# Layer 0 feed-forward: seven block products for gate and up, and a separate down pass

## The chip, the cores and the metric

The kernel runs on one core of a Trainium2 chip. The metric is the device time of one execution in microseconds. Engines are named as in the profile: PE (TensorE), PEld (its weight loads), DVE (VectorE), ACT (ScalarE), POOL (GpSimd), SP (the queue that issues all DMAs here).

## What is computed

Two layers over 512 latent tokens and 256 context tokens of width 1024, in fp32. Layer 0 mixes with differential attention, layer 1 with grouped-query attention; each is followed by a SwiGLU feed-forward with 2816 hidden columns, and adaLN shifts, scales and gates come from small sums over `ada_w`:

```python
def swiglu(t, w_gu, w_down):
    gate, up = jnp.split(t @ w_gu, 2, axis=-1)
    return (jax.nn.silu(gate) * up) @ w_down

mod = (cond_lat @ ada_w[i] + ada_b[i])         # six vectors per layer; modc the same for the context
x  = x  + g1 * y                               # y from the mixer
x  = x  + g2 * swiglu(modulate(rmsnorm(x, norm2_g[i]), sh2, sc2), ffn_w_gu[i], ffn_w_down[i])
xc = xc + cg2 * swiglu(modulate(rmsnorm(xc, norm2_g[i]), csh2, csc2), ffn_w_gu[i], ffn_w_down[i])  # not in the last layer
```

## The kernel before

Tokens are held in blocks of 128: latent blocks 0 to 3, context blocks 4 and 5, worked through in the order 4, 5, 0, 1, 2, 3. For accuracy every fp32 matrix is split in two parts, a rounded high part (an ACT cast to fp32r) and the rest, the low part (a subtraction on DVE or POOL), and each product is three matmuls: high x high, high x low, low x high (`mm3`, L99). `split` (L85) casts on ACT and subtracts on POOL; `split_psum` subtracts on DVE.

The instruction order on each engine is made when the program is built: a scheduler simulates the program in the order of the source and fills the in-order queues; `tc.issue_after(x)` keeps instructions behind x on their engine. All DMAs go through one queue, L55.

The layer-0 feed-forward is `ffn` (L369). It goes through 22 chunks of 128 hidden columns in 11 pieces of two. For each chunk, `stage` loads 1 MB of gate/up weights into one of three raw buffers and splits them (128x2048 on ACT and POOL), and `gu_mm` (L426) computes gate and up transposed: the weights stand in the array, the tokens stream, 512 latent columns into `psgu` and 256 context columns into `psgc`, over 8 blocks of the contraction and 3 products each: 48 pairs of matmuls a chunk. ACT applies silu, DVE multiplies by up, ACT and DVE split the result. One piece later, `down` (L375) multiplies the 256 hidden values of a piece by their rows of `w_down`: for 6 token blocks and 2 column halves, 6 matmuls of 512 columns into one of two `psP` banks, then DVE multiplies by the gate (L386) and adds to the residual `xt` (L387): 132 evictions. While this runs, `ada_job` (L395) makes the adaLN sums of layer 1: twelve column blocks of 512, each from two 1 MB loads, with DVE accumulations (L223, L225) per contraction block, two sums (latent, context) for the first four column blocks and one for the other eight; then small matmuls (L239, L251) and their evictions (L241, L252).

Before it, `out_proj` (L350) adds the attention output to `xt`; after each token block `after` starts the norm (`norm_a`, L292: Square on ACT, a reciprocal root with DVE steps of 128x1, a scaling), and one block later `norm_b` (L330) transposes on PE, modulates on DVE and ACT (L322, L324), and splits (L327, L328). The last two blocks' norms are done by `mid`, inside the first chunk. After the feed-forward, `g_weights` (L1011) has split the key/value weights of layer 1 into the buffers `c` and `d`, and `g_proj` multiplies block after block by them (`psgkv`).

PSUM has eight banks: `psS` twice two, `psP` two, `psT` two. SBUF pools are stacks at two sides; pool `h0p` at the right holds the buffers c, d and e, two of 8 KB a partition each, 48 KB a partition in all, in which the input of the first projection, the attention output and then the feed-forward's weight splits live.

## Time and profile before

| | us |
|---|---|
| median of three runs | 1748.36 |
| lowest, highest | 1746.21, 1749.71 |
| span of the profiled execution | 1742.5 |
| of it: layer-0 feed-forward, first gate/up matmul to first key/value matmul of layer 1 | 606.4 |
| PE, DVE, POOL, ACT busy, share of the span | 95%, 71%, 44%, 39% |

The profiled execution's own time is not shown beside its span; the three runs lie 4 to 7 us above the span. A matmul's busy time includes the end of its pipeline and so overlaps its neighbours'; the distance from start to start says what a matmul costs in a stream. A row's idle time is that of the engine just before the instruction, with what ended it.

### The profile page before, as it was taken

The page shows a single profiled execution, that of the slowest core. Times are in us where ns is not written, and L with a number is a line of the kernel's source. Part 1 is how long each engine was busy: PE and PEld are TensorE (multiplying, and loading weights), DVE is VectorE, ACT ScalarE, POOL GpSimd, SP SyncE. Part 2 cuts the span into 40 slices and gives each one's busy share as a digit, 9 for nine tenths or more (in the row PEclk, how much of TensorE's full clock was granted, in tenths as well). Part 3 has the DMA queues.
Part 4 walks back from the last instruction along what each step waited for, and adds up shares of the span by engine and source line. Part 5 has one row for each costly group of instructions (what it writes and reads, how often), then busy time and mean ns, then how long its engine had stood idle before and what let it go on. Part 6 is the DMA issues. An engine that isn't in the chain of part 4 may idle for free.

```text
span 1742.5 us, 23575 instructions
## 1 busy us (share of the span) xinstructions
PE 1657.0 (95%) x8934; PEld 1403.6 (81%) x8934; DVE 1237.5 (71%) x2016; ACT 673.0 (39%) x1491; POOL 767.6 (44%) x702
## 2 busy tenths in 40 slices
PE   5899999989998999999999999999999999999998
PEld 2789899975778888887777888778897888888887
DVE  4777888877484488878777555798883467677676
ACT  4667767677444121111211022364673522222120
POOL 2687666664645242223232233174435344354340
PEclk8899999999999999999999999999999999999999
DMA  8311111129523133355333221021203133233311
GB/s 303 102 55 38 46 46 58 34 75 336 195 73 121 49 121 111 107 169 169 122 119 99 73 73 40 25 74 48 73 25 120 36 105 103 73 97 99 95 49 49
DMA packets 162435, 165.81 MB, mean 95 GB/s; under 512 B 5097, under 2 KB 120186, under 8 KB 162322
## 3 DMA queue, kind: packets, MB, share of 16 engines
q1 hardware_dynamic: 162322, 164.31, 29.5%
q8 instruction: 70, 1.15, 0.3%
q14 instruction: 43, 0.35, 0.1%
HBM read 159.81 MB, written 4.48 MB: 94 GB/s over the span
## 4 chain that ended last, share of the span: by engine, by line
PE 68%; DVE 18%; ACT 4%; DMA 4%; POOL 3%; issue 2%; SPq 0%; DVEq 0%; ACTq 0%; POOLq 0%
PE psgu L433 24%; PE psgc L433 5%; PE psd L100 5%; PE psd L102 5%; PE psd L101 5%; DVE adacc L225 3%; DMA adaw<-in_ada_w_dram 3%; PE psp L100 2%; PE psp L102 2%; PE psp L101 2%; DVE adacc L223 2%; DVE x L387 2%; DVE xd L386 1%; PE pso L100 1%; PE pso L102 1%
## 5 line engine op out<-in xcount | busy, mean ns | idle before, releaser
L93 POOL TENSOR_TENSOR gul<-gu,guh 128x2048 fp32r<-128x2048 f32 x44 | 211.6, 4809 | 419.6 <-ACT guh L86 419.6
L386 DVE TENSOR_TENSOR xd<-psd,gate 128x512 f32<-128x512 f32 x220 | 151.1, 687 | 202.7 <-PE psd L102 202.5
L387 DVE TENSOR_TENSOR x<-x,xd 128x512 f32<-128x512 f32 x220 | 274.4, 1249 | 5.5
L86 ACT CAST guh<-gu 128x2048 fp32r<-128x2048 f32 x44 | 83.9, 1906 | 403.8 <-PE psgu L433 234.4
L91 POOL TENSOR_TENSOR dl<-wd,dh 128x1024 fp32r<-128x1024 f32 x44 | 120.9, 2768 | 146.1 <-ACT dh L86 146.1
L433 PE MATMUL psgu<-h3latl,guh 128*128 128x512 f32 (+1 forms) x384 | 144.5, 377 | 1.1 <-POOL h3latl L328 1.1
L433 PE MATMUL psgu<-h3lath,gul 128*128 128x512 f32 (+1 forms) x384 | 144.4, 376 | 0.0
L433 PE MATMUL psgu<-h3lath,guh 128*128 128x512 f32 (+1 forms) x384 | 144.3, 377 | 0.0
L433 PE MATMUL psgu<-h2lath,guh 128*128 128x512 f32 (+1 forms) x368 | 142.1, 386 | 0.0
L433 PE MATMUL psgu<-h2lath,gul 128*128 128x512 f32 (+1 forms) x368 | 141.8, 385 | 0.0
L433 PE MATMUL psgu<-h2latl,guh 128*128 128x512 f32 (+1 forms) x368 | 141.8, 385 | 0.0
L100 PE MATMUL psd<-dh,ah 128*128 128x512 f32 x264 | 106.0, 402 | 16.2 <-DVE xd L386 12.1
L102 PE MATMUL psd<-dh,al 128*128 128x512 f32 x264 | 104.8, 397 | 0.0
L101 PE MATMUL psd<-dl,ah 128*128 128x512 f32 x264 | 104.5, 396 | 0.0
L433 PE MATMUL psgc<-h2ctxh,gul 128*128 128x256 f32 x352 | 100.2, 285 | 0.4 <-POOL gul L93 0.4
L433 PE MATMUL psgc<-h2ctxh,guh 128*128 128x256 f32 x352 | 100.1, 284 | 0.0
L433 PE MATMUL psgc<-h2ctxl,guh 128*128 128x256 f32 x352 | 99.6, 283 | 0.0
L225 DVE SCALAR_TENSOR_TENSOR adacc<-adaw,cond,adacc 128x512 f32<-128x512 f32 x112 | 97.5, 896 | 1.3
L100 PE MATMUL psp<-dwh,h0lath 128*128 128x384 f32 x256 | 88.9, 347 | 7.6 <-DVE vl L97 7.6
L101 PE MATMUL psp<-dwl,h0lath 128*128 128x384 f32 x256 | 88.9, 347 | 0.0
L102 PE MATMUL psp<-dwh,h0latl 128*128 128x384 f32 x256 | 88.8, 347 | 0.0
L433 PEld LDWEIGHTS psgu<-h3latl,guh 128*128 128x128 f32 x384 | 72.2, 188 | 15.8 <-POOL h3latl L328 1.3
(389 smaller groups left out, 4669.1 us busy)
## 6 DMA issues: line engine op xcount, KB each, us to landing
adaw<-in_ada_w_dram SPq DMA_DIRECT2D x48, 1024.0 KB
gu<-in_ffn_w_gu_dram SPq DMA_DIRECT2D x88, 512.0 KB
wd<-in_ffn_w_down_dram SPq DMA_DIRECT2D x22, 1024.0 KB
dw<-in_diff_w_in_dram SPq DMA_DIRECT2D x48, 256.0 KB
x<-in_x_dram SPq DMA_DIRECT2D x8, 512.0 KB
wo<-in_diff_w_out_dram SPq DMA_DIRECT2D x4, 1024.0 KB
gw<-in_gqa_w_in_dram SPq DMA_DIRECT2D x4, 1024.0 KB
wo<-in_gqa_w_out_dram SPq DMA_DIRECT2D x4, 1024.0 KB
```

Source lines behind the costliest of these rows:

```text
L86: S.copy(hi, src)
L91: G.tensor_sub(lo[:, ns], src[:, ns], hi[:, ns])
L93: G.tensor_sub(lo[:, :, ns], src[:, :, ns], hi[:, :, ns])
L100: PE.matmul(ps, lhi, rhi, start=start, stop=False)
L101: PE.matmul(ps, lhi, rlo, start=False, stop=False)
L102: PE.matmul(ps, llo, rhi, start=False, stop=stop)
L223: V.tensor_scalar(acc, w[:, k, :], c, None, op0=ALU.mult)
L225: V.scalar_tensor_tensor(acc, w[:, k, :], c, acc, op0=ALU.mult, op1=ALU.add)
L386: V.tensor_mul(tmp, ps, gates[g][:, s, cs])
L387: last_v[0] = V.tensor_add(xt[tb][:, cs], xt[tb][:, cs], tmp)
L433: last[0] = PE.matmul(o, w_[:, k, us], act.t[kind][x_].k(k, sl_), start=(k == 0 and x_ == 0 and w_ is whi), stop=(k == KC - 1 and w_ is wlo))
```

## The change

Layer 1 is left as it is; layer 0's feed-forward is written anew as two passes.

First pass (`ffn_up`). The tokens are two halves of 384 columns, blocks 4, 5, 0 and blocks 1, 2, 3. For each chunk, the 2x2 blocks of weights (gate and up, by lower and upper half of the contraction) times the 2x2 blocks of activations (contraction half by token half) are computed by seven products of sums instead of eight (Winograd's form of Strassen's scheme). `Forms` makes the seven activation forms once: b11, b21 (first half), b22, and the sums t1 to t4, which need both halves, each split in high and low; the forms take the place of the attention output and of other buffers. `prep` makes the seven weight forms of a chunk, seven products ahead: four sums or differences of 128x512 on POOL, seven ACT casts, six low parts on DVE and one on POOL. Each product is 12 matmuls of 384 columns. Four of the products add on to one PSUM bank, with ACT copies (c1, c2) and a DVE addition (u2) between; DVE adds the copies, multiplies silu(gate) by up, and the result goes to DRAM (`a0`) unsplit. The adaLN sums move into this pass: one step every two products (`ada_step`), with loads of half the size into two buffers of their own.

Second pass (`ffn_down`). For each half, all 22 chunks are added up in six PSUM banks, and each of the 12 results is evicted once. Activations are read back from DRAM and split (128x1536), the weights of down are loaded and split for each half. Norms of layer 1 follow the blocks of each half.

Buffers change with it: `h0p` becomes two 24 KB tiles, used in turn by the projection's input, the attention output, the forms t1 to t4 and at last the activations of down (`a2t`, in the place of t1 and t2, held until the last matmul of down). Only then the pool with c, d, e opens in the same 48 KB, in the order c, e, d; the key/value weights go to e and d, so the first high part lies within `a2t`'s 24 KB.

```diff
+    class Forms:
...
+        def put(self, name, j, src, eng):
...
+            S.copy(t[:, 0, :, cs], src)
+            last_v[0] = eng.tensor_sub(t[:, 1, :, cs], src, t[:, 0, :, cs])
...
+        def done(self, xs, tb, banks=None):
+            ht = norm_mod(xs, norm_t(xs, tb, self.l, 1, banks), tb, self.l, 1)
...
+            if half == 0:
+                self.put("b11", j, lo, V)
+                self.put("b21", j, hi, G)
+            else:
+                b11, b21 = self.ht[0, j]
+                self.put("b22", j, hi, G)
+                V.tensor_sub(b11, lo, b11)
+                self.put("t1", j, b11, V)
+                V.tensor_sub(lo, hi, lo)
+                V.tensor_sub(hi, hi, b11)
+                self.put("t2", j, hi, G)
+                V.tensor_sub(b21, b21, hi)
+                self.put("t3", j, lo, V)
+                self.put("t4", j, b21, G)
...
+    RHS = {1: "b11", 2: "b21", 3: "b22", 4: "t4", 5: "t1", 6: "t2", 7: "t3"}
+    PLEAD = 7
+
+    def product_order():
+        o = [(0, 1), None, (0, 2), (1, 1), (1, 2), None, (2, 1), (2, 2), (0, 5), (0, 6), (0, 3), (0, 7), (1, 5), (0, 4), (1, 6), (1, 3), (1, 7)]
+        o += [(1, 4), (2, 5), (2, 6), (2, 3), (2, 7)]
+        for h in range(3, NHC):
+            o += [(h, 1), (h - 1, 4), (h, 2), (h, 5), (h, 6), (h, 3), (h, 7)]
+        return o + [(NHC - 1, 4)]
+
+    def ffn_up(l, F, ev_tile, st_tile, a_dram, adds, mid, step):
...
+        def prep(hc, n):
+            w = raw[hc]
+            r11, r12, r21, r22 = [w[:, k : k + 4, u : u + P] for u in (0, P) for k in (0, 4)]
+            s1 = st_tile(hc)
+            if n == 5:
+                adds[0].tensor_add(s1, r21, r22)
+                adds[1].tensor_sub(r21, r11, r21)
+            elif n == 6:
+                adds[2].tensor_sub(r11, s1, r11)
+            elif n == 3:
+                adds[3].tensor_sub(r12, r12, r11)
+            src = {1: r11, 2: r12, 5: s1, 6: r11, 3: r12, 7: r21, 4: r22}[n]
...
+            S.copy(t[:, 0], src)
+            (G if n == 4 else V).tensor_sub(t[:, 1], src, t[:, 0])
+            if n == 4:
+                load(hc + 3)
...
+            for k in range(4):
+                for a_, b_ in ((0, 0), (0, 1), (1, 0)):
+                    last_m[0] = PE.matmul(
+                        ps, w[:, a_, k, :], x[:, b_, k, :],
+                        start=(n in (1, 2, 5) and k == 0 and a_ + b_ == 0),
...
+            if n == 1:
+                S.copy(c1, ps)
+            elif n == 2:
+                V.tensor_add(g1, ps, c1)
+                S.activation(g1, g1, AF.Silu)
+            elif n == 5:
+                S.copy(c5, ps)
+            elif n == 6:
+                S.copy(c2, ps)
+            elif n == 3:
+                V.tensor_add(g2, ps, c2)
+                S.activation(g2, g2, AF.Silu)
+            elif n == 7:
+                V.tensor_add(u2, ps, c5)
+                last_v[0] = V.tensor_mul(g2, g2, u2)
+                puts.append((i, hc, 1, g2))
+            else:
+                last_v[0] = V.tensor_mul(g1, g1, ps)
+                puts.append((i, hc, 0, g1))
+            step(i)
...
+    def ffn_down(l, xt, halves, g, a_dram, a_tile, banks, lo_eng, after):
...
+        PREP, LOAD, TAIL = 3, 5, 2
...
+            for k in range(NHC - TAIL):
+                load(half * NHC + k + LOAD)
+                for tb in tbs:
+                    for ch in range(2):
+                        mms(k, tb, ch)
+                prep(half * NHC + k + PREP)
...
+                    V.tensor_mul(tmp, ps[tb][ch], gates[g][:, s, cs])
+                    last_v[0] = V.tensor_add(xt[tb][:, cs], xt[tb][:, cs], tmp)
+                    after(tb, ch)
...
+    HALVES = ([4, 5, 0], [1, 2, 3])
...
+    def ada_work(js):
...
+            for k0 in range(0, KC, 2):
+                w = half_slab(f"adw{j}_{k0}").rearrange("p (k n) -> p k n", k=2)
+                dma(w, ada_w[1, k0 * P : (k0 + 2) * P, j * 512 : j * 512 + 512].rearrange("(k p) n -> p k n", p=P))
+                yield
+                with tc.issue_after(last_v[0].ins):
...
+    def ada_step(i):
+        while ada_n[0] < (i - 14) // 2:
+            ada_n[0] += 1
+            next(ada_it, None)
...
-    ffn(0, xt, h2, tb_order, (0, 1), tags0, lambda: after(None, True), lambda: gate_load(1), [mk_ada1(j) for j in (0, 1, 2, 3, 6, 7, 8, 9, 4, 5, 10, 11)], after0)
...
+    ffn_up(
+        0, F0, ev0, lambda hc: st0[:, hc % 2], a0, (G, G, G, G), mid0, ada_step)
...
+    ffn_down(
+        0, xt, HALVES, (0, 1), a0, lambda i: a2t[:, i % 2 * 8 * TH : i % 2 * 8 * TH + 8 * TH],
+        (("S", "S", "P"), ("T", "S", "S")), G, lambda tb, ch: after(tb) if ch else None)
...
-        wt = g_weights(GQA_HEADS * GQA_DH, "kv", "cd")
+        wt = g_weights(GQA_HEADS * GQA_DH, "kv", "ed")
```

## Rows read from the trace of the kernel before

**Rows 1.** Busy shares of the page; a window: us, busy by engine, clock, DMA share.
```profile
PE 1657.0 (95%) x8934; PEld 1403.6 (81%) x8934; DVE 1237.5 (71%) x2016; ACT 673.0 (39%) x1491; POOL 767.6 (44%) x702
...
522.75:1129.19 606.44, 583.16 (x3091) 493.13 (x3090) 419.07 (x518) 120.78 (x165) 179.93 (x55) 0.99 0.32 100
```

**Rows 2.** Timeline of PE (start, us, what): the stage's first matmul, layer 1's first.
```profile
522.75 0.36 PE L433 MATMUL psgc<-h2ctxh,guh 128*128 128x256 f32 x1
...
1129.19 0.47 PE L100 MATMUL psgkv<-gwhkv,h1ctxh 128*128 128x512 f32 x1
```

**Rows 3.** Timeline of PE: ends of a run of gate/up pairs, of down matmuls, of 384-column matmuls.
```profile
559.97 0.39 PE L433 MATMUL psgu<-h2lath,gul 128*128 128x512 f32 x1
...
583.14 0.39 PE L433 MATMUL psgu<-h2lath,gul 128*128 128x512 f32 x1
...
584.42 0.39 PE L100 MATMUL psd<-dh,ah 128*128 128x512 f32 x1
...
586.99 0.39 PE L102 MATMUL psd<-dh,al 128*128 128x512 f32 x1
...
153.10 0.34 PE L102 MATMUL psp<-dwh,h0latl 128*128 128x384 f32 x1
...
155.35 0.33 PE L100 MATMUL psp<-dwh,h0ctxh 128*128 128x384 f32 x1
```

**Rows 4.** PE's waits: by line in the stage, in the timeline, and in the table of waits.
```profile
L100 PE MATMUL psd<-dh,ah 128*128 128x512 f32 x264 | 106.0, 402 | 16.2 <-DVE xd L386 12.1 <-DVE mod L241 4.1
...
533.67 1.97 PE L307 MATMUL pt<-ident,xs01f 128*128 128x128 f32 x8 [4.87 <-DVE m_n L112]
...
PE psd L100 <- DVE xd L386: 12.1, 10, 2.2
```

**Rows 5.** Down's evictions by tile, 520 to 1130: ns min/median/max, first and last start.
```profile
L386 DVE TENSOR_TENSOR xd<-psd,gate x132: 676/691/694, 586.0 to 1129.1; 128x512 f32<-128x512 f32 x132
L387 DVE TENSOR_TENSOR x<-x,xd x130: 676/692/5061, 587.0 to 1127.8; 128x512 f32<-128x512 f32 x130
```

**Rows 6.** Timelines of DVE and POOL where they meet (start, us).
```profile
525.99 3.26 DVE L105 TENSOR_TENSOR m_n<-m_n,r_n 128x1 f32<-128x1 f32 x1 [1.21 <-ACT r_n L114]
...
524.19 5.04 POOL L93 TENSOR_TENSOR gul<-gu,guh 128x2048 fp32r<-128x2048 f32 x1
...
1132.33 5.00 POOL L328 TENSOR_TENSOR h1ctxl<-xs10f,h1ctxh 128x512 fp32r<-128x512 f32 x1 [7.10 <-ACT h1ctxh L327]
...
626.77 8.04 DVE L225 SCALAR_TENSOR_TENSOR adacc<-adaw,cond,adacc 128x512 f32<-128x512 f32 x12
```

**Rows 7.** Durations by tile (min/median/max) and, the last row, by line.
```profile
L328 POOL TENSOR_TENSOR h2latl<-xs01f,h2lath x2: 1274/1284/1294, 537.8 to 541.0; 128x512 fp32r<-128x512 f32 x2
...
L91 POOL TENSOR_TENSOR dl<-wd,dh x22: 2331/2756/3116, 521.8 to 1064.0; 128x1024 fp32r<-128x1024 f32 x22
...
L479 DVE TENSOR_TENSOR sil<-sil,psgc x22: 404/413/423, 545.1 to 1102.3; 128x256 f32<-128x256 f32 x22
...
L86 ACT CAST gwhkv<-gwkv 128x512 fp32r<-128x512 f32 x8 | 4.5, 615 | 31.8 <-PE psgu L433 31.8
```

**Rows 8.** adaLN: chain of work (start, us), and DVE's waits for its loads.
```profile
635.04 1.34 PE ps_adac L239 x12
...
912.50 0.96 PE ps_adar L251 x2
...
741.87 6.27 DMA adaw<-in_ada_w_dram
...
DVE adacc L223 <- DMA adaw<-in_ada_w_dram: 12.6, 3, 5.9
```

**Rows 9.** Timeline of DVE: first and last of the norms' steps at the start.
```profile
509.74 0.75 DVE L297 TENSOR_SCALAR xs01g<-x,r_n 128x1024 f32<-128x1024 f32 x1
...
541.50 1.37 DVE L328 TENSOR_TENSOR h2latl<-xs01f,h2lath 128x512 fp32r<-128x512 f32 x1 [1.45 <-ACT h2lath L327]
```

**Rows 10.** POOL's splits of the key/value weights by tile.
```profile
L91 POOL TENSOR_TENSOR gwlkv<-gwkv,gwhkv x8: 1287/1301/1834, 1073.6 to 1105.8; 128x512 fp32r<-128x512 f32 x8
```

More of the change, by code (lines that the diff above doesn't have):

```diff
@@ L298, in norm_a, with norm_t @@
         return xs
-    def norm_t(xs, tb, l, which):
+    def norm_t(xs, tb, l, which, banks=None):
         pts = []
@@ new lines, in finish_to @@
+    def finish_to(l, which, act):
+        return lambda xs, tb: norm_b(xs, tb, l, which, *act.blk(tb))
+    HALVES = ([4, 5, 0], [1, 2, 3])
+    TH = 3 * P
+    form_view = lambda t: t.rearrange("p (x k n) -> p x k n", x=2, k=4)
+    F0 = Forms(0, HALVES, {
+        n: form_view(bfp.tile([P, 8 * TH], F32R, tag=n, name=f"hf0{n}", bufs=1)) for n in ("b11", "b21", "b22")})
+    after = mk_after(0, 1, lambda tb: mp.tile([P, D], F32, tag="m", name=f"xs01{tb}") if tb not in (2, 3) else half_slab(f"xs01{tb}"), lambda xs, tb: F0.done(xs, tb, "T" if tb in (2, 3) else None), 1, NLAT - 1)
```

269 lines of the change are left out of this document (225 added, 44 removed).

## The prediction

> **What bounds the kernel now.** I read the page's busy shares first, then the windows by stage, then TensorE's timeline inside the stage that the diff rewrites, and last its idle time and what ends it. The page gives PE 95% of the span [rows 1]; busy matmul time overlaps itself, so pitches (start to start) tell more. Layer 0's feed-forward runs from its first gate/up matmul at 522.75 us to the first matmul of layer 1 at 1129.19 us: 606.4 us, a third of the span, at a granted clock of 0.99, the 2.4 GHz level [rows 1, 2]. In a quiet stretch the pair of a 256-column and a 512-column matmul repeats 66 times between 559.97 and 583.14, 0.351 us a pair; eleven steps of the down matmuls take 2.57 us, 0.2336 us each [rows 3]. One hidden chunk (128 hidden columns) has 48 pairs, 16.85 us; 22 of them make 370.7 us. Down has 11 x 12 x 6 = 792 matmuls, 185.0 us. So 556 of the 606 us are matmuls at their own pitch: the stage is bound by TensorE. The other 50 us are adaLN matmuls, transposes, a 4.9 us wait for the last norms at the start, and waits of down for its PSUM evictions (16.2 us of idle before L100) while DVE does adaLN sums [rows 4].
>
> **What is removed and added on TensorE.** Gate and up become seven products instead of eight blocks. A product is 4 x 3 matmuls of 384 columns, so 22 x 7 x 12 = 1848. The same form exists in the q/k/v projections: thirteen steps from 153.10 to 155.35 are 2.25 us, 0.1731 us each [rows 3]. That is 2.08 us a product, 14.54 us a chunk and 319.9 us in all, 50.8 us less than 370.7. Per column 384 is no worse than the old mix (0.451 ns against 0.457). Down keeps its 792 matmuls: 185.0 us. The adaLN matmuls stay: twelve records in 1.34 us, so 96 make 10.7 us, and two row matmuls in 0.96, so eight make 4 us [rows 8]. Forty transposes stay too: eight took 1.97 us with a wait inside [rows 4], so 10 us at most; I take 5. The floor of the new stage is 319.9 + 185.0 + 14.7 + 5 = 525 us, 82 us below 606. All that follows is how much of the 82 is lost again.
>
> **Down's evictions.** Before, 132 times a multiplication from PSUM and an addition to x, 0.69 us each at the median [rows 5]: 182 us of DVE. After, twelve pairs, 17 us. The 16.2 us of idle are gone with them, and this is part of the 82. In their place down loads and splits its weights twice. A 128x1024 subtraction took POOL 2.76 us (median) and TensorE now needs 18 x 0.2336 = 4.2 us for one chunk of one half, so POOL, the slowest of the splitters, is covered with 1.4 us to spare [rows 7]; three chunks of lead cover the loads. I cost this at nothing; without cover it would be 2.8 us at each half.
>
> **The port between DVE and POOL.** This is the main loss. In the trace a DVE instruction on SBUF operands waits while POOL runs one: a 128x1 multiplication took 3.26 us under a 5.04 us POOL subtraction, and a POOL subtraction that takes 1.29 us took 5.00 us under a DVE chain [rows 6]. The DVE multiplications that read PSUM never stretch (676 to 694 ns), the SBUF additions do (up to 5061 ns) [rows 5]. So SBUF work of DVE and POOL adds up; only PSUM-reading DVE work runs beside POOL.
> Ten products in the new loop, 20.8 us on TensorE, cost DVE: 8.6 lo parts of 128x512 at 0.61 (pitch: 0.69 less the overlap of neighbours) = 5.2; evictions of 384 columns, between the 413 ns of 256 and the 691 of 512 [rows 5, 7], 0.475 at pitch, five a chunk = 3.4, of which 2.7 read PSUM. POOL: five instructions of 1.29 us a chunk = 9.2 [rows 7]. The adaLN sums advance by one of twelve column blocks in ten products. The first four blocks carry two sums: 14 accumulations at 0.67 (twelve took 8.04 us) and two starts, 10.3; the other eight carry one, 5.1 [rows 6].
> First four blocks: 5.2 + 3.4 + 10.3 = 18.9 for DVE, with POOL 28.1 if nothing overlaps, 25.4 if all PSUM reads do; TensorE needs 20.8 + 1.7 for adaLN = 22.5. Loss 2.9 to 5.6 per block, 12 to 22 in all. The lead of seven weight preparations does not absorb it, because evictions stand in the same DVE queue: u2 must have left PSUM before the eighth step of the chunk may add to it, one product later. I take 12, since PSUM reads do overlap in the rows.
> Other eight blocks: 13.7 + 9.2 = 22.9, or 20.2 with overlap, against 21.7. So 0 to 10. In addition a half-size adaLN load has only two products (4.2 us) from issue to use. Before, a 1 MB load cost 6.3 us where the chain shows it, and DVE waited three times, 12.6 us [rows 8]. I add up to 8 and take 6 for both together, nearest to half of the 12.6.
> The Trainium skill, page "SBUF — State Buffer", section "SBUF: two separate sides", says that DVE and POOL hold their shared ports exclusively for a whole instruction, and counts DVE instructions with two SBUF inputs among the holders. The rows agree (3.26 and 5.00 us). By that rule the first four blocks cost 12 us and not 0, and the rule speaks against moving more DVE and POOL work beside each other, as this change does.
>
> **The start.** Six products (12.5 us) and two blocks' transposes (2 us) are there to cover the norms of token blocks 2 and 3, so TensorE reaches the first product that needs the second half at about 537. Between 509.74 and 542.87 DVE does some 22 us of norm work in the kernel before, the rest is idle or locked out by POOL's big splits [rows 6, 9]. After, the same stretch has five more 128x512 steps for each of three blocks (9.2), ten lo parts of weights (6.1) and first evictions (1.4): 39 us, so 549. POOL's fifteen short subtractions (19 us), 11 of them beside PSUM reads, add up to 8. The stall is 6 (if block 1's forms fit into idle time) to 22; I take 14. Before's own 4.9 us there is inside the 606.
>
> **The joints.** Up to down: weights and activations of the first chunks can be split some products early, and the last PSUM bank frees in one eviction; 2 us (0 to 6). Between the halves and at the end: 2 (0 to 4). Down to layer 1: before, the key/value weights were split at 1073 to 1106, well ahead. After, their first tile lies in memory that the down activations hold until the last matmul. Four subtractions of 1.30 us [rows 10] then run one by one while TensorE wants 0.7 us a piece, so about 4 us (0 to 8).
>
> **The sum.** 82 - 14 - 12 - 6 - 2 - 2 - 4 = 42 us. The span of 1742.5 becomes 1700; the runs shown are 1746 to 1750, some 4 to 7 us around the span, which the change doesn't touch. So 1748.4 - 42 = 1706 us.
>
> **The rivals.**
> 1. All hidden. The scheduler orders the queues so that the port is shared without loss and the forms are ready. Only the 6 us at the start stay: 82 - 6 = 76, 1672; with a little at the joints 1680. For: eight of the twelve adaLN blocks need 20.2 against 21.7 with overlap. Against: the first four exceed TensorE even then. Chance 0.17.
> 2. The port binds the whole first pass. Nothing overlaps: 22 + 10 + 8 for the pass, 22 at the start, 7 at the joints: 69, leaving 13: 1735. Chance 0.18. By the skill's rule on the shared ports nothing but PSUM reads runs beside POOL, so the rule stands between this rival and the forecast.
> 3. Slower: in-order queues chain the products. Each chunk reuses one PSUM bank for five products, with ACT copies (c1, c2) and DVE additions (u2) between them, and the same queues hold weight casts that wait for POOL. If a cast that waits for POOL stands ahead of a copy, TensorE waits in every chunk. Before, a down matmul waited 1.2 us on average and up to 2.2 for DVE's eviction, ten times [rows 4]. With the 22 us of start and joints, the remaining 60 us are used up at 0.39 us a product. Two waits of 2 us in each of 22 chunks are 88 us: 1748 - 82 + 22 + 88 = 1776. For: the bank is reused within one product's time (2.08 us). Against: ACT has seven casts of 128x512 (615 ns [rows 7]) and five passes of 384 columns, at most 0.6 each, 7.3 us in 14.5, and preparations run six products ahead. Chance 0.12.
>
> **How the numbers follow.** Forecast (1688 to 1724) 0.50, all hidden 0.17, port-bound 0.18, slower 0.12, and 0.03 for landing within 0.2% (3.5 us, about what a measurement of this kernel can tell from no change). Faster 0.85, same 0.03, slower 0.12. For 8 in 10 the range takes in most of the first and second rival: 1674 to 1744. It leaves out the slower case and the very best.
>
> **What would show it.** In the profile after, chunk period on TensorE without adaLN near 14.5 us and 384-column pitch 0.173 us; if the period is longer in quiet chunks too, rival 3. In the first four adaLN blocks longer periods, with DVE additions and POOL instructions stretched beyond 0.69 and 1.29 us; if they stretch but TensorE doesn't idle, rival 1. One idle stretch of 6 to 22 us on TensorE after six products, ended by DVE or a form. Down at 0.2336 us without idle. A gap of up to 8 us at the first psgkv, ended by a split. The prediction is wrong if the loss per chunk is the same with and without adaLN, or if DMA ends most idle time.

## The result, and the profile after

The changed kernel takes 1728.57 us (median of four runs, 1725.67 to 1733.0) against 1748.46 before; the ratio is 0.9883 with a 95% interval of 0.9859 to 0.9908. So 20 us were gained where 42 were forecast. The sign is right and the time lies inside the range, but less than half of the forecast gain came. The profiled execution has a span of 1723.9 us against 1742.5, 18.6 us less, and its own time is 1725.67.

First the borders of the stage, from TensorE's timeline of the kernel after (start, us, what): the first product, the first key/value matmul, the first gate/up matmul of layer 1.

```profile
530.37 1.13 PE L634 MATMUL psu<-hf0b,wf 128*128 128x384 f32 x5
...
1100.94 0.71 PE L100 MATMUL psgkv<-gwhkv,h1ctxh 128*128 128x512 f32 x2
...
1347.65 0.48 PE L489 MATMUL psgu<-h3lath,guh 128*128 128x256 f32 x2
```

Against [rows 2] the 18.6 us divide into four parts.

| stretch | before, us | after, us | difference | forecast |
|---|---|---|---|---|
| start to the stage's first product | 522.75 | 530.37 | +7.6 | 0 |
| the stage, to the first key/value matmul | 606.4 | 570.6 | -35.9 | -46 |
| key/value projection and attention of layer 1 | 235.8 | 246.7 | +10.9 | +4 |
| the rest (layer 1's feed-forward) | 377.5 | 376.2 | -1.3 | 0 |

Next the windows inside the first pass (us from the span's start, length, busy us with instruction counts of PE, PEld, DVE, ACT, POOL, the granted clock of TensorE as a share of 2.4 GHz, DMA share, GB/s).

```profile
530.00:560.00 30.00, 17.33 (x94) 15.89 (x92) 30.00 (x48) 19.41 (x45) 19.98 (x14) 0.78 0.24 71
560.00:600.00 40.00, 35.39 (x186) 34.56 (x187) 26.76 (x33) 15.12 (x30) 25.51 (x15) 0.91 0.39 112
600.00:640.00 40.00, 37.59 (x199) 36.45 (x198) 36.95 (x46) 13.86 (x28) 15.88 (x11) 0.91 0.46 138
640.00:680.00 40.00, 38.11 (x219) 37.34 (x217) 39.76 (x53) 13.92 (x28) 19.12 (x12) 0.96 0.54 157
...
800.00:840.00 40.00, 40.00 (x221) 37.77 (x221) 37.01 (x49) 16.53 (x33) 19.20 (x13) 1.00 0.61 183
```

TensorE idles 17.3 us at the start (530 to 573) and 8.7 us in the rest of the pass, nearly all of that before 741. DVE is full from 530 to 560 and nearly full again to 720, where the adaLN blocks with two sums run. From 760 on only one wait of 0.4 us is left, though adaLN blocks with one sum run there. Up to 720 the clock's mean is below 1.00 in every window: TensorE has four stretches at the lower level, 0.50 or 1.2 GHz (columns as above).

```profile
546.88:567.36 20.48, 9.09 (x32) 7.78 (x31) 18.07 (x31) 13.07 (x27) 15.78 (x9) 0.50 0.19 53
618.56:625.39 6.83, 6.83 (x26) 6.83 (x26) 3.78 (x7) 1.98 (x4) 1.30 (x1) 0.50 0.28 90
649.28:652.69 3.41, 3.41 (x12) 3.41 (x11) 3.41 (x7) 0.66 (x2) 0.63 (x1) 0.50 1.07 319
683.42:686.83 3.41, 3.41 (x12) 3.41 (x13) 3.41 (x7) 0.53 (x1) 1.18 (x1) 0.50 0.86 277
```

The first begins behind a wait of 2.2 us and has the waits of 7.1 and 3.7 in it; the others follow waits of 1.2, 0.4 and 0.8, of 0.4 and 0.8, and of 4.0 us. TensorE works 9.1 us in the first and 13.7 in the others, all of it at half speed, so 4.5 us are lost at the start and 6.8 in the rest of the pass.

The waits of TensorE in this pass by what ended them (us in total, times, longest), in answer to [rows 4]:

```profile
PE pt L319 <- DVE xs L334: 7.1, 1, 7.1
PE psu L634 <- DVE g L658: 4.0, 1, 4.0
PE psc L634 <- ACT tf L360: 3.7, 1, 3.7
PE psu L634 <- POOL tf L361: 2.8, 1, 2.8
PE ps_adac L248 <- DVE adacc L1231: 2.7, 4, 0.8
```

And what TensorE does undisturbed, from its timeline: one product begins 2.08 and 2.12 us after the one before. [Rows 3] gave 2.08.

```profile
895.10 2.24 PE L634 MATMUL psu<-tf,wf 128*128 128x384 f32 x12
897.18 2.28 PE L634 MATMUL psu<-hf0b,wf 128*128 128x384 f32 x12
899.30 2.10 PE L634 MATMUL psc<-hf0b,wf 128*128 128x384 f32 x11
```

Down's 132 evictions are twelve now (by tile: ns min/median/max, first and last start), and TensorE waits 1.8 us for them in all, where [rows 4] had 12.1, or 16.2 with the adaLN steps in DVE's queue:

```profile
L739 DVE TENSOR_TENSOR xd<-psd,gate x12: 673/684/692, 993.7 to 1099.9; 128x512 f32<-128x512 f32 x12
```

At the border to layer 1 stands a gap that was not there before. In order of time, from the timelines of POOL, DVE, ACT and PE:

```profile
1100.34 11.96 POOL L91 TENSOR_TENSOR gwlkv<-gwkv,gwhkv 128x512 fp32r<-128x512 f32 x8 [4.92 <-ACT gwhkv L86]
1105.06 2.96 DVE L1371 TENSOR_TENSOR gtab<-rope 128x256 f32<-128x256 f32 x2
1112.68 0.20 ACT L113 ACTIVATE r_n<-m_n 128x1 f32<-128x1 f32 x1 [5.12 <-DVE m_n L112]
1115.42 1.09 PE L319 MATMUL pt<-ident,xs 128*128 128x128 f32 x8 [2.83 <-DVE xs L306]
1117.94 0.38 ACT L1303 COPY gtemp<-psgkv 128x256 f32<-128x256 f32 x1
1118.19 0.40 ACT L96 CAST vvh<-psgkv 128x256 fp32r<-128x256 f32 x1
1125.33 1.72 DVE L344 TENSOR_TENSOR h1latl<-xs,h1lath 128x512 fp32r<-128x512 f32 x1 [2.45 <-ACT h1lath L343]
1128.18 0.74 DVE L97 TENSOR_TENSOR vvl<-psgkv,vvh 128x256 fp32r<-128x256 f32 x2
1128.73 0.77 PE L100 MATMUL psgkv<-gwhkv,h1lath 128*128 128x512 f32 x1 [10.42 <-DVE vvl L97]
```

The two PSUM banks of `psgkv` hold blocks 4 and 5. ACT's copy out of the first of them stands in its queue behind the norm steps of the last blocks, and DVE's `vvl` behind their low parts. In the longer gap DVE itself idles 3.8 us, 2.45 of it for ACT's cast of a last block, while `vvl`, whose input `vvh` was cast at 1118.2, stands behind: what holds the bank is the place of `vvl` in the queue. TensorE idles 2.8 and 10.4 us, and its next twelve matmuls start 0.43 us apart instead of 0.23, the lower clock level, until 1133.99, which costs another 2.5 us. That is 15.7 us of loss in one place.

### The profile page after: what moved, and what is told of

Same layout as the page of the kernel before. It is cut to its first block, busy times and chain, and to the rows that moved or that the text cites. A ratio compares the mean times of both kernels' runs of the same rounds, so it can differ in the third digit from the quotient of the medians.

```text
span 1723.9 us, 23682 instructions
## 1 busy us (share of the span) xinstructions
PE 1618.3 (94%) x8622; PEld 1411.0 (82%) x8622; DVE 1200.6 (70%) x1979; ACT 775.8 (45%) x1710; POOL 893.1 (52%) x818
## 4 chain that ended last, share of the span: by engine, by line
PE 73%; DVE 14%; ACT 4%; POOL 3%; DMA 3%; issue 3%; SPq 0%; DVEq 0%; ACTq 0%; POOLq 0%
PE psgu L489 14%; PE psu L634 10%; PE psd L102 5%; PE psd L101 5%; PE psd L100 5%; PE psc L634 4%; DVE adacc L1231 2%; PE psp L100 2%; PE psp L102 2%; PE psp L101 2%; DMA adaw<-in_ada_w_dram 2%; PE pso L100 2%; PE pso L102 1%; PE pso L101 1%; DVE wf L604 1%
## 5 line engine op out<-in xcount | busy, mean ns | idle before, releaser
L93 POOL TENSOR_TENSOR gul<-gu,guh 128x2048 fp32r<-128x2048 f32 x22 | 102.2, 4645 | 181.5 <-ACT guh L86 181.5
L634 PE MATMUL psu<-tf,wf 128*128 128x384 f32 x756 | 144.8, 340 | 4.8 <-POOL tf L361 2.8
L443 DVE TENSOR_TENSOR x<-x,xd 128x512 f32<-128x512 f32 x88 | 143.9, 1637 | 2.3
L100 PE MATMUL psp<-dwh,h0h 128*128 128x384 f32 x384 | 134.1, 349 | 11.4 <-DVE vl L97 8.6
L634 PEld LDWEIGHTS psu<-tf,wf 128*128 128x128 f32 x756 | 133.4, 190 | 7.0 <-POOL tf L361 3.1
L101 PE MATMUL psp<-dwl,h0h 128*128 128x384 f32 x384 | 133.3, 347 | 0.0
L102 PE MATMUL psp<-dwh,h0l 128*128 128x384 f32 x384 | 132.9, 347 | 0.0
L1231 DVE SCALAR_TENSOR_TENSOR adacc<-adw,cond,adacc 128x512 f32<-128x512 f32 x112 | 116.7, 1058 | 6.2 <-DMA adw<-in_ada_w_dram 5.9
L604 DVE TENSOR_TENSOR wf<-gu,wf 128x512 fp32r<-128x512 f32 x110 | 104.7, 965 | 5.4 <-ACT wf L603 5.4
L634 PE MATMUL psu<-hf0b,wf 128*128 128x384 f32 x504 | 99.1, 344 | 4.0 <-DVE g L658 4.0
```

Of the source, the lines that this page charges most:

```text
L93: G.tensor_sub(lo[:, :, ns], src[:, :, ns], hi[:, :, ns])
L100: PE.matmul(ps, lhi, rhi, start=start, stop=False)
L101: PE.matmul(ps, lhi, rlo, start=False, stop=False)
L102: PE.matmul(ps, llo, rhi, start=False, stop=stop)
L443: last_v[0] = V.tensor_add(xt[tb][:, cs], xt[tb][:, cs], tmp)
L604: (G if n == 4 else V).tensor_sub(t[:, 1], src, t[:, 0])
```

## The experiments

Each edit is shown against the kernel it was made on. "First pass" is from the start of the first product to the start of the last, "projection" from the first key/value matmul to the last, "attention" from there to layer 1's first gate/up matmul; all are from TensorE's timeline of the profiled execution, and for the kernel after they are 383.9, 53.2 and 193.5 us. Before the change the projection took 40.5 and the attention 195.4.

**The changed kernel again.** No edit.

> The changed kernel once more, unaltered. It tells what of its 7.6 us before the feed-forward is of the kernel and what of one execution: last output-projection matmul at 529 us against 522 before. Theory (a property of its instruction order): the 2.7 us that stand between 184 and 408 us and the 5 us more at the joint of attention and output projection come back within 0.5 us each. Rival (one execution's DMA luck): the 2.7 us, which begin with a first adaLN load 1.1 us late at 17 us, are gone or changed by over 1 us. Total 1726 to 1733, as before.

1730.0 us, ratio 0.9888 [0.9872, 0.9903]. The stage began at 530.0 and the first pass took 385.1. The mean over a head (`pm`, a matmul of layer 0's mixer) that stood at 183.6 came at 183.0, so the late start looked like a property of the kernel. But later kernels with the same order up to there had it at 178.2 and at 180.4 (`kv_banks`, `forms_dve`) and began the stage at 526.0 and 526.4. One execution's start therefore scatters by 5 us, and my theory was too strong. What does repeat is the joint of attention and output projection: the matmuls of its first part (`pso0p`, first to last) take 32.6 to 33.0 us in every profile after the change and 29.0 in the one before.

**Additions on DVE.**

```diff
-        0, F0, ev0, lambda hc: st0[:, hc % 2], a0, (G, G, G, G), mid0, ada_step)
+        0, F0, ev0, lambda hc: st0[:, hc % 2], a0, (V, V, V, V), mid0, ada_step)
```

> The four additions of 128x512 by which the weight forms of each chunk are made run on DVE instead of POOL. On POOL one takes 1.28 us, on DVE 0.69. Theory 1 (SBUF work of DVE and POOL shares one port, so their sum binds): 4 x 0.6 = 2.4 us less a chunk; the waits at the start (17 us) shrink by 3 to 6 and those of the four adaLN blocks with two sums (8 us) by 2 to 5; 1718 to 1725. Rival (DVE's own queue binds): DVE gets 2.8 us more a chunk, the waits in the first pass grow by 3 to 15 us, 1731 to 1745.

1710.4 us, ratio 0.9771 [0.9755, 0.9787]: 18 us faster, more than expected. DVE got more to do, and the waits for it nearly vanished: idle time of the pass outside the start fell from 8.7 to 1.8 us, the start's from 17.3 to 15.6, and the first pass took 368.1, 15.8 less; behind 570 it has no stretch at the lower clock level any more. The windows of this kernel, to be held against those above:

```profile
560.00:600.00 40.00, 36.57 (x193) 36.06 (x194) 28.39 (x43) 17.32 (x34) 13.28 (x7) 0.88 0.38 112
600.00:640.00 40.00, 39.44 (x231) 38.95 (x230) 37.86 (x60) 15.49 (x30) 4.59 (x3) 1.00 0.53 152
640.00:680.00 40.00, 40.00 (x241) 39.70 (x240) 40.00 (x68) 16.80 (x33) 3.70 (x3) 1.00 0.57 174
```

From 600 on POOL's busy time is about a quarter of what it was, and DVE, as full as before, does 68 instructions where it did 53. The groups of DVE by shape (600 to 900; busy us, mean ns of one) say why: first the kernel after,

```profile
L1231 DVE SCALAR_TENSOR_TENSOR adacc<-adw,cond,adacc 128x512 f32<-128x512 f32 x109 | 112.4, 1048 | 6.2 <-DMA adw<-in_ada_w_dram 5.9
...
L644 DVE TENSOR_TENSOR g<-psu,c 128x384 f32<-128x384 f32 x19 | 10.4, 547 | 0.6 <-PE psu L634 0.6
```

then the one with the additions on DVE.

```profile
L1231 DVE SCALAR_TENSOR_TENSOR adacc<-adw,cond,adacc 128x512 f32<-128x512 f32 x107 | 84.8, 801 | 5.9 <-DMA adw<-in_ada_w_dram 5.8
```

An accumulation on SBUF operands takes 1048 ns in the mean beside a busy POOL and 801 with POOL nearly idle. The addition that reads PSUM (L644) takes 547 and 546. So DVE's busy time in the kernel after contains waiting for POOL. The rival (DVE's own queue length) is out: DVE has more instructions and is less in the way.

**Most adaLN terms left out.**

```diff
-                            else:
+                            elif k0 + k == KC - 1:
                                 V.scalar_tensor_tensor(acc, w[:, k, :], c, acc, op0=ALU.mult, op1=ALU.add)
```

> Six of the eight contraction terms of each adaLN sum of layer 1 are left out (the loads, the first and the last term, the small matmuls stay), so layer 1 gets wrong shifts, scales and gates. Theory 1 (DVE's adaLN additions, beside POOL, make TensorE wait in the four blocks with two sums): the waits between 600 and 683 us fall from 8 us to under 2 and the clock there rises from 0.87-0.98 to 1.00; nothing changes before 570; 1717 to 1722. Rival (the products are chained by their own evictions and casts): less than 3 us gained.

1713.3 us, ratio 0.9783 [0.9762, 0.9805]; first pass 368.9, idle outside the start 0.4 us, start 18.4. Taking work from DVE makes the pass 15.0 us shorter, nearly what taking it from POOL gave. POOL keeps all its additions here, so its own pace did not make the waits either. It is the sum of the two that stood against TensorE, not either one, and the product chain of rival 3 has no part in it.

**adaLN paced by size.**

```diff
-        while ada_n[0] < (i - 14) // 2:
+        while ada_n[0] < min((i - 14) // 3, 20) + max((i - 74) // 2, 0):
```

> The changed kernel (additions on POOL) with the adaLN sums paced by their size: a step every three products in the four blocks with two sums, every two in the others; nothing is left out. By the port's count DVE and POOL together then need 8.6 x 1.5 + 10.3 + POOL 9.2 x 1.5 = 37 us for fifteen products of 31.2 + 1.7 on TensorE in such a block. Theory 1 (rate: sums of DVE and POOL work against TensorE's time): the waits between 600 and 683 us fall from 8 to 3 or less, and the clock there rises; 1718 to 1724. Rival (not the rate but the start's backlog and the queues' order): less than 3 us gained, or the waits only move on to later products; 1726 to 1731.

1732.0 us, ratio 0.9906 [0.9891, 0.9921]: no gain. In the blocks it was made for, the forecast came: between 600 and 683 the waits fell from 7.6 to 3.2 us and the clock's mean rose to 1.00 (first the kernel after, then this one; the third line is TensorE's).

```profile
600.00:683.00 83.00, 75.70 (x416) 73.79 (x414) 79.72 (x102) 28.69 (x56) 35.12 (x23) 0.94 0.49 143
600.00:683.00 83.00, 79.69 (x461) 78.09 (x460) 73.48 (x96) 31.78 (x62) 38.06 (x26) 1.00 0.49 144
905.63 0.80 PE L102 MATMUL psd<-wd_0x,a2t 128*128 128x512 f32 x1 [4.15 <-DVE a2t L693]
```

Down's first matmul starts 372.2 us after the first product instead of 377.9 (some 1 us of it because two adaLN matmuls come later). But the sums now run to the end of the pass: waits of 1.4 and 1.9 us come at 695 and 729, down's first activations are split late, its matmuls wait 4.15 us at 901, and the next ten start 0.43 us apart, the lower clock level. The rate was a lever in the pass, and the rest of the sums gave the gain back where down begins.

**Key/value weights early.** The weights go to the second 24 KB tile and the two adaLN buffers, and are split ahead of the last two chunks of down.

```diff
+    kvt = h0p.tile([P, KC * T], F32R, tag="h", name="kvt").rearrange("p (x k n) -> p x k n", x=3, k=4)
+    kvl = [half_slab(f"kvl{i}", F32R).rearrange("p (k n) -> p k n", k=2) for i in range(2)]
...
             prep(half * NHC + NHC - TAIL + PREP)
+            if half:
+                kv_weights()
...
-        wt = g_weights(GQA_HEADS * GQA_DH, "kv", "ed")
+        wt = wkv
```

> Only the place of the key/value weights of layer 1 is changed: they go to memory that is free when the second half of down runs (the second 24 KB tile, and the two 4 KB adaLN buffers), and are split before the last two chunks of down instead of after its last matmul. Theory 1 (their late memory holds ACT with eight casts and POOL with 12 us of subtractions at 1100 to 1112, and DVE's norm steps are locked out under them): the 10.4 us gap of TensorE at 1118 and the 2.8 us gap at 1113 go, layer 1's attention is 8 to 11 us shorter, 1718 to 1721 us in all. Rival (the norms of the last blocks alone are late, because down's last evictions come in one burst): the weights are early, but the gap before the last key/value blocks stays, 0 to 4 us gained, 1725 to 1729.

1737.3 us, ratio 0.9931 [0.9906, 0.9956]: 7 us slower than the changed kernel. The weights were ready, key/value matmuls even ran among the last of down, and still TensorE waited:

```profile
1122.19 3.47 PE L319 MATMUL pt<-ident,xs 128*128 128x128 f32 x16 [6.29 <-DVE xs L306]
1128.19 0.44 PE L1367 MATMUL ptk<-ident,gtemp 128*128 128x128 f32 x2 [1.99 <-ACT xs L336]
1131.20 0.77 PE L100 MATMUL psgkv<-kvt,h1lath 128*128 128x512 f32 x1 [2.58 <-DVE vvl L97]
```

The first rows end with the norms of the last blocks, the last with the bank. From the end of the first pass to the last key/value matmul it is 233.1 us against 238.0. So my reason for the term (late memory, then four subtractions in a row) was worth some 5 us at most, and theory 1's 8 to 11 fell. The 5 us were lost elsewhere. The attention behind took 204.3 us; 9.5 of its 10.8 us more are 6.1 of waits, the longest of 3.8 us for the last keys, and 3.4 lost in 6.8 us at the lower clock level. The first pass took 389.4, though its instructions stand in the same order on all four engines; it spent 44 us at the lower level instead of 34, so most of that difference is one execution's clock and not the edit.

**More banks.** On the additions on DVE.

```diff
+            if nm == "kv" and tb in (0, 1):
+                if tb == 0:
+                    psS.append(ps2("psgkvS"))
+                ps = psS[0][:, tb, :]
+            else:
-            ps = psb(f"psg{nm}{tb}", "P")
+                ps = psb(f"psg{nm}{tb}", "P")
```

> On top of the four additions on DVE (1710 us, span 1711.7): the key/value products of token blocks 0 and 1 go to the free pair of PSUM banks instead of waiting for the two banks of blocks 4 and 5. In the run before, TensorE stands 2.8 us at 1097 and 10.4 us at 1103, the second until DVE's low part of the values (L97) has left the first bank; ACT's copy of that bank is queued behind the norms of the last two token blocks. Theory 1 (two banks and in-order queues make the gap; the weights are in time): the 10.4 us go, 6 to 11 us gained, 1700 to 1705. Rival (the norms of the last blocks are the end of the chain whatever TensorE does meanwhile): the gap moves ahead of the last two blocks, 0 to 4 us gained.

1711.3 us, ratio 0.9785 [0.977, 0.9799], no change. The 10.4 us became 4.4 and the projection, 53.3 us with the additions on DVE, 48.5; but the attention grew from 193.5 to 199.8. There POOL, DVE and PE meet in one line each:

```profile
1182.42 5.22 POOL L93 TENSOR_TENSOR wol<-wo,woh 128x512 fp32r<-128x512 f32 x4 [1.49 <-ACT woh L86]
1182.57 5.21 DVE L1325 SCALAR_TENSOR_TENSOR gtemp<-guq,r_gq,gtemp 128x128 f32<-128x128 f32 x4
```

Four small DVE steps, which took 1.6 us ten microseconds earlier, end with POOL's run of four, and TensorE waits 5.12 us at 1184.9. The gain was real and was given back at the next run of POOL.

**Key/value low parts on DVE.** On the additions on DVE.

```diff
-                    split(hi[:, k, :], lo[:, k, :], w[:, k, :])
+                    S.copy(hi[:, k, :], w[:, k, :])
+                    (V if nm == "kv" else G).tensor_sub(lo[:, k, :], w[:, k, :], hi[:, k, :])
```

> On top of the four additions on DVE (1710 us, span 1711.7): the eight low parts of the key/value weights run on DVE (about 0.65 us each) instead of POOL, where they were one run of 12.0 us (1100.34 to 1112.30 in the changed kernel) during which DVE's rope tables took 9.4 us, against 0.67 a step in the kernel before, and the norms of the last token blocks came late. Theory 1 (POOL's run locks DVE out and so delays the norms): DVE needs 5.2 + 2.9 = 8 us for what took 12, the norms and the gap of 2.8 + 10.4 us shrink by 3 to 5 us, 1705 to 1708. Rival (DVE's own queue: more work on DVE makes the norms later): 0 to 4 us slower, 1710 to 1715.

1708.8 us, ratio 0.9763 [0.9746, 0.978]. The gap of 2.8 us is gone, the one of 10.4 is 10.3, two waits of 0.8 came; the projection took 50.5 us. By itself this edit takes 2.8 us off the projection and the pair of banks 4.8; the next run has both.

**Both, and the output weights on DVE too.** On the additions on DVE, with the last two edits and

```diff
-                split(hi[:, ks, :], lo[:, ks, :], w[:, ks, :], 2)
+                S.copy(hi[:, ks, :], w[:, ks, :])
+                for ns in (slice(0, 256), slice(256, 512)):
+                    (V if nm == "1" else G).tensor_sub(lo[:, ks, ns], w[:, ks, ns], hi[:, ks, ns])
```

> Four edits together: the additions on DVE; key/value products of blocks 0 and 1 in the free PSUM pair; the low parts of the key/value weights on DVE; those of layer 1's output weights on DVE too, since a POOL run of four (5.22 us at 1182.42) took four rotary steps of DVE from 1.27 to 5.21 us there and TensorE waited 5.12 us, just what the second pair of banks had gained. Theory 1 (each gain is real and was given back at the next run of POOL): 8 to 13 us below the additions alone, 1697 to 1703. Rival (layer 1's attention is held by DVE's whole work, about 90% busy there, so that what is gained early is waited for later): 0 to 4 us gained, 1706 to 1711.

1709.8 us, ratio 0.977 [0.9752, 0.9789]. The projection took 41.7 us, about as before the change (40.5): together the two edits take off 11.6 us, 4 more than each by itself adds up to. The attention took 204.4. This looked like the rival, an attention held by its own bound.

**Both, the output weights left on POOL.**

> The additions on DVE, the key/value products of blocks 0 and 1 in the free PSUM pair, and the low parts of the key/value weights on DVE; the output weights' low parts stay on POOL. With those on DVE as well the key/value projection took 41.7 us (40.5 before the change, 53.2 after it) and the attention behind it 204.4 instead of 193.5. Theory 1 (DVE's added work for the output weights gave the gain back): the projection stays near 42 and the attention goes to 194 to 199; 1701 to 1706. Rival (the attention is held by DVE's whole work or by the order of its queue; what is gained in the projection is waited for): attention 202 to 206, 1708 to 1711.

1703.6 us, ratio 0.9742 [0.9727, 0.9756]. Projection 41.7, attention 199.1. So at least 5 of the 11 us that the attention had grown by were the added DVE work of the output weights. From the last matmul of down to layer 1's feed-forward it is 242.5 us against 248.6. Most of the attention's remaining growth, 5.6 us, goes with one wait for the last keys, just behind the projection, and 3.4 us at the lower clock level after it:

```profile
1126.96 10.15 POOL L1337 TENSOR_TENSOR gwl<-gw,gwh 128x512 fp32r<-128x512 f32 x8
1134.84 0.45 PE L1359 MATMUL ptk<-ident,gtemp 128*128 128x128 f32 x1 [4.03 <-DVE gtemp L1325]
```

POOL's next run, the low parts of the query weights, stands over DVE's steps for these keys: two steps of 128x128 (L1320) that took 0.62 us at 1123 take 2.59 at 1130.8.

**Form parts on DVE.** On the additions on DVE, `b21`, `b22`, `t2` and `t4` are put with V.

```diff
-                self.put("b21", j, hi, G)
+                self.put("b21", j, hi, V)
```

> On top of the four additions on DVE (1710 us): the twelve low parts of activation forms that POOL makes at the start (b21, b22, t2, t4) also go to DVE, 1.28 us each on POOL, about 0.65 on DVE. Theory 1 (shared port, the sum binds): 12 x 0.6 = 7 us less work in 530 to 575, of which some lies beside PSUM reads; the 15.6 us of waits there fall by 3 to 6, 1704 to 1708. Rival (DVE is busy for 30.0 of the 30 us from 530 to 560, and its own queue is what binds now): the waits grow by 3 to 8 us, 1713 to 1719.

1710.4 us, ratio 0.9788 [0.9772, 0.9804], no change; the start idles 15.8 us against 15.6. What DVE no longer waits for POOL, it now works itself; that is my reading, and no run parts the two.

**Weight parts of the first chunks on ACT.** On the additions on DVE.

```diff
+            if hc < 3 and n != 4:
+                S.copy(t[:, 1], src)
+            else:
-            (G if n == 4 else V).tensor_sub(t[:, 1], src, t[:, 0])
+                (G if n == 4 else V).tensor_sub(t[:, 1], src, t[:, 0])
```

> On top of the four additions on DVE (1710 us): the low parts of the weight forms of the first three chunks (18 subtractions of 128x512 on DVE, 0.61 apart, 11 us, nearly all of them before 565 us) are replaced by plain copies on ACT, so that these chunks' products are wrong. DVE was busy for 30.0 of the 30 us from 530 to 560. Theory 1 (DVE's work, norms of two blocks and forms and weights in one queue, is the start's bound): the four waits of 7.6, 2.7, 4.0 and 1.4 us fall by 6 to 11 us together; 1700 to 1705. Rival (the chain of one norm, from transposes over modulation to forms, is the bound): less than 3 us gained.

1715.7 us, ratio 0.98 [0.9781, 0.982]: slower. DVE's share of 530 to 560 fell to 23.2 us, but ACT is then busy for 29.1 of the 30, the norms' ACT steps stand behind the copies, and three loads of activation tables, 1.28 us each, fall into the stretch where the kernel it is built on has one. The start idles 16.7 us. This one only moved the bound and tells nothing of DVE's share.

**Form sums left out.** On the additions on DVE.

```diff
-                V.tensor_sub(b11, lo, b11)
                 self.put("t1", j, b11, V)
-                V.tensor_sub(lo, hi, lo)
-                V.tensor_sub(hi, hi, b11)
                 self.put("t2", j, hi, G)
-                V.tensor_sub(b21, b21, hi)
                 self.put("t3", j, lo, V)
```

> On top of the four additions on DVE (1710 us, span 1711.7): the four sums of activation forms of blocks 1 to 3 (twelve subtractions of 128x512 on DVE, 0.6 apart, 7 us) are left out, the forms t1 to t4 being split from their first operand, so gate and up are wrong. Moving work between the engines left the start's waits at 16 to 17 us (POOL's additions to DVE 15.6, POOL's form parts to DVE 15.8, DVE's weight parts to ACT 16.8). Theory 1 (the start is a chain, and these sums are a part of it): the waits between 530 and 575 fall by 5 to 9 us, 1701 to 1705. Rival (the norms of the last two blocks alone, behind the output projection's last evictions, make the chain): under 2 us gained, 1708 to 1711.

1704.6 us, ratio 0.976 [0.9743, 0.9777]. The start idles 12.9 us, 2.8 less; the first pass is 3.6 us shorter, and the rest of the 6 us lies within the scatter of the executions' start. Neither theory holds: the sums are a fifth of the wait. DVE's timeline here shows another part:

```profile
539.29 1.24 DVE L105 TENSOR_TENSOR m_n<-m_n,r_n 128x1 f32<-128x1 f32 x1
...
543.88 1.22 DVE L106 SCALAR_TENSOR_TENSOR m_n<-m_n,r_n 128x1 f32<-128x1 f32 x1
...
548.35 0.15 DVE L107 SCALAR_TENSOR_TENSOR r_n<-m_n,r_n 128x1 f32<-128x1 f32 x1
...
550.16 0.74 DVE L306 TENSOR_SCALAR xs<-x,r_n 128x1024 f32<-128x1024 f32 x1
```

Three steps of one number per partition take 9 us, because weight forms stand between them in the queue.

**Order of the start.** On the additions on DVE; `last_f` is DVE's last low part of an activation form.

```diff
-            while nprep <= min(i + PLEAD, len(preps) - 1):
-                prep(*preps[nprep])
+            while nprep <= min(i + (2 if i < 8 else PLEAD), len(preps) - 1):
+                with tc.issue_after(last_f[0].ins) if 7 <= nprep < 16 else nullcontext():
+                    prep(*preps[nprep])
```

> On top of the four additions on DVE (1710 us, span 1711.7): no work is moved to another engine and none left out; in DVE's queue the weight forms that are not needed before the second half's first product (the eighth to sixteenth) stand behind the activation forms instead of between the steps of the norms of blocks 2 and 3. In the run that leaves the form sums out, the chain of four small norm steps (L105, L106, L107, L306) went over 11 us, 539.3 to 550.2, with weight parts in between. Theory 1 (the order in DVE's queue makes the start's wait): the waits of 15.6 us between 530 and 565 fall to 6 to 11; 1701 to 1706. Rival (the wait is DVE's whole work before the first product of the second half, whatever its order, and the weight forms put back are late for the next products): the waits only move, 0 to 2 us gained, 1708 to 1712.

1708.4 us, ratio 0.9777 [0.976, 0.9793]. The start idles 12.6 us and the first pass takes 366.2, 1.9 less. That is small but repeats: the five kernels above that have this pass unedited, with the additions on DVE, take 367.7 to 369.4 (`adds_dve`, `kv_banks`, `kv_lo_dve`, `best1`, `best2`), the three with the new order 366.0 to 366.7. The waits are other ones now:

```profile
541.81 1.33 PE L319 MATMUL pt<-ident,xs 128*128 128x128 f32 x8 [1.36 <-DVE xs L334]
547.15 0.69 PE L637 MATMUL psc<-tf,wf 128*128 128x384 f32 x1 [4.01 <-ACT tf L360]
551.66 3.53 PE L637 MATMUL psc<-tf,wf 128*128 128x384 f32 x11 [3.82 <-DVE tf L361]
```

The first transposes of the second half stand 15.1 us behind the first product instead of 20.5 (the 7.6 us wait for `xs` is 1.4), and then the forms bind; another 3.4 us go to casts of the weight forms that were put back, as the rival said. Order is worth a fifth of the wait. That the larger rest is the amount of work on DVE before the second half's first product is likely but not shown.

**Spilled heads' low parts on DVE.** On the additions on DVE.

```diff
-                split(hi.k(h), lo.k(h), w[:, h - h0_, sl])
+                S.copy(hi.k(h), w[:, h - h0_, sl])
+                V.tensor_sub(lo.k(h), w[:, h - h0_, sl], hi.k(h))
```

> On top of the four additions on DVE (1710 us): the low parts of the six spilled heads of the attention output run on DVE instead of POOL, where they stand in one 13 us run at 453.70 behind the last head's mean, while before they began at 440.89 and were spread. Theory (that run delays the first part of the output projection, and with it the stage's start, 530 us against 522.75): the copies of its sums (ACT, 467.4 to 476.5) come 4 to 7 us earlier and the first product at 524 to 527; 1704 to 1707. Rival (the gate and x loads that are issued ahead of the projection's weights, 446 to 457, delay the weights): the first product stays at 530 to 531.

1712.3 us, ratio 0.9795 [0.978, 0.9809]. The stage began at 530.6, and the first part of the output projection took 32.6 us against 33.0. My theory on the joint fell. The rival's loads were not tried alone.

**What gained, together.** The order of the start and the key/value low parts on DVE, on the additions on DVE:

> The additions on DVE, the later weight forms behind the activation forms in DVE's queue, and the low parts of the key/value weights on DVE (the last alone: 1709 us). Theory: the gains of the start add to it, 1699 to 1705. Rival (the start's waits only move): 1707 to 1710.

1705.3 us, ratio 0.9753 [0.9737, 0.9769]. And with the free bank pair as well:

> All edits that gained, together: the additions on DVE, the later weight forms behind the activation forms in DVE's queue, the key/value products of blocks 0 and 1 in the free PSUM pair, the low parts of the key/value weights on DVE. Against the same without the queue order (1703.6 us) the order of the queue was worth 2.6 us in the first pass. Theory (the two places are apart and add): 1699 to 1703. Rival (the queue order's 2.6 us are lost again later): 1703 to 1706.

1700.0 us, ratio 0.9722 [0.9682, 0.9762]: 48 us below the kernel before, 28 below the change as it stood, the lowest median here. First pass 366.7, start 12.2, projection 42.5, attention 197.2. The order's part in the first pass is 1.9 us and not the 2.6 expected from. The two places seem to add, but its runs (1697.7 to 1705.7) overlap those of the same kernel without the order of the start (1700.0 to 1704.6).

## Why the prediction was wrong in size

**What failed, in short.** The terms of the sum counted idle time only. They add up to 40 us, and TensorE idles 44 in the same places. But the time it then works at the lower clock level, some 15 us in the pass, down and the key/value projection, was in no term, and neither were the 7.6 us before the stage. With these, 82 - 44 - 15 - 8 = 15 us would be left, against 18.6 measured. By place, the terms mis-sized are the start (14 forecast, 21.8 measured) and the joint from down to layer 1 (4 forecast, 10.9 measured), and at the joint the mechanism was wrong too.

**TensorE's floor.** Right. A quiet product is 2.08 us, and down's matmuls take 182.7 us in place of 185.0. The 82 us were there. So were the evictions' 16.2 us, and the only wait of down for its splits is 0.5 us long.

**The port.** The mechanism and nearly the size are right. Forecast were 12 + 6 = 18 us for the adaLN blocks; with either engine relieved the pass is 15 to 16 us shorter. Only the way of payment differs: 8.7 us are idle time, and the rest is mostly the 6.8 us lost at the lower clock level, a term that I did not have. Nearly all of it stands in the first four blocks (15 us against 12); the other eight, priced at 6, lost next to nothing. That the total came near is therefore partly luck. The Trainium skill, page "SBUF — State Buffer", section "SBUF: two separate sides", has the shared port as an exclusive lock for a whole instruction; 1048 ns beside 801 for the same accumulation, and the unchanged 547 and 546 ns of the PSUM readers, agree. I had the fact and the price on POOL and DVE (1.28 and 0.69 us) before me and read them only as a cost. That the same additions cost the port half as much on DVE follows from them and was worth 18 us.

**The start.** This is the term mis-sized most. 14 us (6 to 22) were forecast; it idles 17.3 and loses 4.5 more to the lower clock, 21.8 in all, so more than half of what is missing is the clock. The queue also mixes weight forms with the steps of the norms: of the idle time the order was worth 3 us (2 of the pass), the sums of forms 3. What makes the other 10 us of idle time is open.

**Down to layer 1.** The step failed, not only its size. I priced four late subtractions at 4 us. The weights were nearly in time: the matmuls of blocks 4 and 5 that stand ahead of the first gap run from 1100.94 to 1112.6 nearly at the pitch of down, 0.2 us late at most where a low part is used first. What I left out is what the split queues behind itself: a 12 us run on POOL, under which DVE's rope tables and norm steps stretch, and two banks whose evictions stand behind those norms in ACT's and DVE's queues. That cost 13 us of the projection (53.2 against 40.5). I had put down that the norms of the second half follow down's last blocks, but not that these norms now come in one burst, while before they were spread: their transposes start 7 to 9 us apart from 1120.0 to 1151.6, and after the change two blocks' stand 2 us apart at 1115.4 and 1117.3. Neither the run on POOL nor the banks makes the loss by itself: lifted alone they give 2.8 and 4.8 us, together 11.6.

**Before the stage.** I called it unchanged. It was 7.6 us later in the profiled execution. Some 3.8 us repeat in every profile, at the joint of attention and output projection; the remainder is within the 5 us by which the start of single executions differs. The cause of the 3.8 is open: it is not the run of low parts on POOL.

**The joints.** Up to down has a wait of 0.4 us, 0.5 and 1.8 stand at the start of the second half, 1.8 and 0.5 before the end: 4 forecast, 5.0 measured, and 1.7 more at the lower clock.

**The rivals.** All hidden was wrong and port-bound too far: its 1735 is above the 1728.6 measured, which lies between it and the forecast. The in-order chain of rival 3 did not appear between products, but it did appear at the key/value joint, where I had not looked for it. Of the misses, the start has 8 us, the key/value joint 7, the repeating part before the stage 3.8, the other joints 3. Against them stand 2 to 3 us less at the port and 2 less of down's matmuls. The first pass holds some 5 us more of small losses that I did not place.

## What to carry to other kernels

Where two engines share a port, count their work as one sum, and give each instruction to the engine that holds the port for the shorter time, even if that engine looks full: its busy time may be waiting. When a restructured loop moves evictions and norms into one burst, follow the in-order queues past the joint and ask which PSUM bank is released behind that burst. A gain made ahead of a busy stretch has to be followed to the end of that stretch before it is counted. And a wait of TensorE is to be priced with the time that it then works at the lower clock level: here 44 us of waits came with some 15 us of it.

## What was not expected of the hardware

A 10.4 us idle stretch of TensorE was followed by twelve matmuls of 512 columns 0.43 us apart, then by 0.23 again; the 5 us at the lower level cost 2.5 us beyond the idle time itself. Waits of 1.2 us and less were followed by a stretch at the lower level too (618.6 to 625.4). A POOL run of four subtractions (5.22 us) held four DVE steps of 128x128 for 5.21 us. Kernels whose instructions stand in the same order up to that point reached the first matmul of the output projection between 438.7 and 443.9 us (and then the feed-forward between 526.0 and 531.1); the first part of that projection itself took 32.6 to 33.0 us in all of them. So the length of a joint can be read to half a microsecond from one trace, while the start of the stage cannot.
